# Hybrid decoder trunk: the low halves of twelve up tiles change engine, and a gate multiplication walks its operands in another order

## The chip, the cores and the metric

The kernel runs on one core of one Trainium2 chip. A time is the device time of one execution in microseconds (us), and what counts is the median of several runs. The kernel before takes 2404.12 us, the median of three runs between 2401.31 and 2413.12.

## The reference

Two layers, each a mixer followed by a PEER feed-forward block, over 256 positions of width 1024. The change touches the PEER block alone. Cut to what matters:

```
q = (xt @ w_query).reshape(T, 8, 2, 128)
s1, s2 = q[:, :, 0] @ subkeys[0].T, q[:, :, 1] @ subkeys[1].T
(v1, i1), (v2, i2) = top_k(s1, 16), top_k(s2, 16)
top, pos = top_k(all 256 sums v1 + v2, 16)
idx  = take_along_axis(i1 * 128 + i2, pos)
gate = softmax(top)
act  = gelu(einsum('thkd,td->thk', u_table[idx], x))
y    = einsum('thk,thkd->td', gate * act, v_table[idx])
```

There are 16384 experts, 128 by 128. The kernel does not gather rows of the tables: it multiplies all experts with all positions and lets the gate be zero where an expert was not chosen.

## The kernel before, in words

Products are made at more than the precision of one pass: every float32 operand is split into a high half, rounded to the multiplier's type, and a low half, the remainder, and three matmuls (high by high, low by high, high by low) stand for one product.

**Streaming (`stream`, lines 77 to 89).** Every weight tile of 128 x 1024 (512 KB) goes the same way. SyncE's queue loads it into one of four `raw` buffers; ScalarE casts it into one of three `hi` buffers (line 84); the low half, `raw - hi`, goes into one of three `lo` buffers (line 88), on the engine that the caller names. On VectorE that is one instruction of 1024 elements a partition, on GpSimd two of 512. `project` (lines 238 to 251) streams one tile and issues its 24 matmuls of 256 columns (lines 247 to 249). With three `hi` and `lo` buffers, the cast of tile n can begin only when TensorE is through with tile n-3.

**The order of the work.** The program is written for a framework that schedules: it takes the instructions as the program emits them, keeps a reckoning of its own of how long each takes, and gives each engine a fixed queue. An instruction that is emitted late may come early in its engine's queue if in that reckoning the engine has nothing earlier that is ready. On the chip each engine then runs its queue strictly in order. `tc.keep_in_program_order` holds single instructions in their program place on their engine.

**The PEER block (`peer`, lines 890 to 1059), in program order:**
- Queries: 16 tiles of `w_q`, low halves on GpSimd. After each head, `scores` (lines 928 to 942) makes the two score tables on TensorE and searches the top 16 on VectorE (lines 922 to 926, and the 16 x 16 sums of line 940).
- Up tiles: 128 tiles of `uT`, one `up(e)` for each (lines 953 to 955). `up` projects the tile and puts its Gelu (ScalarE, line 955) into `H`. Tiles 0 to 43 have their low halves on GpSimd, tiles 44 to 127 on VectorE.
- After `up(23)` the program emits the gate arithmetic on VectorE (lines 968 to 986). A softmax begins with an exponential on ScalarE (line 969, held in program order, so behind the Gelu of tile 23), whose result lines 970 to 973 use. Lines 974 to 978 take indices apart (977 and 978 convert the two index tables to float). Then come two times four rounds that look up the chosen keys: compare (line 983), multiply (line 985) and reduce (line 986), each 1024 elements a partition. All rounds use one buffer, so each of these 24 operations depends on the one before.
- `up(24)` to `up(43)`; then `sel` and the gates are transposed on TensorE (lines 989 to 995), held in program order. After that `up(44)` to `up(63)`.
- `up(64)` to `up(127)`, with `weigh(0, t8)` in between, 32 times: one-hot tables of eight positions on VectorE (lines 1011 to 1016), 16 small matmuls into a PSUM buffer (line 1020), and the multiplication of the up tiles by these gates (line 1023). `H[half]` holds 64 tiles by 256 positions a partition; line 1023 reads and writes a block of 64 tiles by 8 positions of it, so neighbouring tiles lie 256 elements apart and neighbouring positions 1. The gates in PSUM lie as 8 positions by 64 tiles.
- The accumulation over 128 tiles of `vt` (lines 253 to 277, matmuls of 512 columns in line 262), low halves on VectorE, with `weigh(1, t8)` between its first 60 steps.

Of the kernel before, what the change touches and what calls it, by code (L numbers as in the profile page):

```python
# [17 lines left out]
OP = mybir.AluOpType  # L18
# [21 lines left out]
GATE_SCALE = 2.0 ** 15  # L40
# [5 lines left out]
def trunk(ctx, tc, x, xT, w_in, w_br, w_out, w_q, skT, uT, vt, prm, lora, g2, v1, v2, rgw, w_uq, w_ukv,  # L46
          lnp, rope, out):
    nc = tc.nc
    V, A, G, T = nc.vector, nc.scalar, nc.gpsimd, nc.tensor
# [8 lines left out]
    def nm(s):  # L58
        uid[0] += 1
        return f"{s}{uid[0]}"  # L60
# [10 lines left out]
    def psm():  # L71
        return ps("sm", 2)
# [63 lines left out]
    with tc.tile_pool(name="setup", bufs=1) as sb:  # L136
        def t8(n):
            return sb.tile([P, L, 4], F32, tag=n, name=n)
        la = pr[:, :, PC["la"]:PC["la"] + 4]
        ab, e, q, w, w2, acc, rl = (t8(n) for n in ("ab", "e", "q", "w", "w2", "acc", "rl"))  # L140
# [89 lines left out]
    def drain(g):  # L230

        while True:
            try:
                next(g)
            except StopIteration as e:
                return e.value

    def project(src, eng=None):
        return drain(projecting(src, eng))

    def projecting(src, eng=None):
        hi, lo = stream(src, eng)
        h3, l3 = hi.rearrange("p (k c) -> p k c", k=8), lo.rearrange("p (k c) -> p k c", k=8)
        pt = pmm()[:, :S]
        xth, xtl = state["xth"], state["xtl"]
        for k in range(8):
            T.matmul(pt, h3[:, k, :], xth[:, k, :], start=(k == 0), stop=False)  # L247
            T.matmul(pt, h3[:, k, :], xtl[:, k, :], start=False, stop=False)  # L248
            T.matmul(pt, l3[:, k, :], xth[:, k, :], start=False, stop=(k == 7))  # L249
            yield  # L250
        return pt
# [638 lines left out]
    def peer(l, hp):  # L890
# [14 lines left out]
        H = [early.enter_context(tc.tile_pool(name=f"h{l}", bufs=1)).tile([P, 64, S], F32, tag="H0", name=nm("H"))]  # L905
# [9 lines left out]
        def nxt(k, lst):  # L915
            cyc[k] = cyc.get(k, -1) + 1
            return lst[cyc[k] % len(lst)]
# [33 lines left out]
            prev = (h, q)  # L951

        def up(e):
            p = project(uT[l, e], G if e < 44 else V)
            A.activation(H[e // 64][:, e % 64, :], p, AF.Gelu_apprx_tanh)  # L955

        up(0)
        scores(*prev)
        for e in range(1, 24):
            up(e)  # L960
# [18 lines left out]
        for f in range(2):  # L979
            for h4 in range(4):  # L980
                hs = slice(4 * h4, 4 * h4 + 4)
                t = nxt("map", maps)
# [4 lines left out]
        for e in range(24, 44):  # L987
            up(e)
        for b in range(2):
            p = psm()  # L990
# [15 lines left out]
        def weigh(half, t8):  # L1006
            oh = hp.tile([P, 8, 64, 2], F16, tag="oh", name=nm("oh"), bufs=2)
            eq = hp.tile([P, 8, 32, 2], F16, tag="eq", name=nm("eq"), bufs=2)
            go = hp.tile([P, 2, 8, 32, 2], F16, tag="go", name=nm("go"), bufs=2)
            tt = slice(8 * t8, 8 * t8 + 8)  # L1010
            V.tensor_tensor(oh, iota16[:, None].to_broadcast([P, 8, 64, 2]),  # L1011
                            ix[:, 1, tt, None, :].to_broadcast([P, 8, 64, 2]), op=OP.is_equal)
            V.tensor_tensor(eq, iota16[:, None, 32 * half:32 * half + 32].to_broadcast([P, 8, 32, 2]),
                            ix[:, 0, tt, None, :].to_broadcast([P, 8, 32, 2]), op=OP.is_equal)
            for i in range(2):
                V.tensor_tensor(go[:, i], eq, gp[:, i, tt, None, :].to_broadcast([P, 8, 32, 2]), op=OP.mult)  # L1016
            p = psm()
            for j in range(8):
                for i in range(2):
                    T.matmul(p[:, j * 64:(j + 1) * 64], oh[:, j].rearrange("p a b -> p (a b)"),  # L1020
                             go[:, i, j].rearrange("p a b -> p (a b)"), start=(i == 0), stop=(i == 1))
            hv = H[half][:, :, tt].rearrange("p e t -> p t e")
            V.scalar_tensor_tensor(hv, p.rearrange("p (t e) -> p t e", t=8), 1 / GATE_SCALE, hv, op0=OP.mult, op1=OP.mult)  # L1023

        def weigh_some(half, e):

            for t8 in range(min(e * 32 // 60, 32), min((e + 1) * 32 // 60, 32)):
                weigh(half, t8)
# [107 lines left out]
```

## Time and profile before

| | |
|---|---|
| median of 3 runs | 2404.12 us (2401.31 to 2413.12) |
| the profiled execution, its own time | 2409.22 us |
| its span in the trace | 2407.5 us |
| TensorE busy | 2264.9 us, 94% |
| VectorE busy | 1761.2 us, 73% |
| ScalarE busy | 1035.3 us, 43% |
| GpSimd busy | 679.4 us, 28% |

In the rows below PE is TensorE's matmuls, PEld its weight loads, DVE VectorE, ACT ScalarE, POOL GpSimd. "L88" is line 88 of the kernel. Times start at the beginning of the span. Matmuls are pipelined, so a busy PE says only that work was at hand.

### The profile page before, as it was taken

Reading aid. Unit: us, or ns where it says so; the run is one execution under the profiler, and the core shown is the slowest. Engines: PE = TensorE matmul, PEld = TensorE weight load, DVE = VectorE, ACT = ScalarE, POOL = GpSimd, SP = SyncE. Lnnn points to the kernel's source line nnn. Section 1 sums busy time; section 2 is a strip of 40 time slices with the busy share of each in tenths; the row PEclk is TensorE's granted clock in tenths of the full one; section 3 lists DMA queues with packets and bytes.
Section 4 is the critical chain, followed back from the end, with each engine's and each line's share of the span. In section 5 each row is a group of like instructions: output and inputs, shape, how many; then the busy total and the mean of one; then the engine's idle time right before and its main releaser. Section 6 shows DMA issues by size and latency. Waiting matters only on the chain.

```text
span 2407.5 us, 42363 instructions
## 1 busy us (share of the span) xinstructions
PE 2264.9 (94%) x17092; PEld 2066.4 (86%) x17092; DVE 1761.2 (73%) x2956; ACT 1035.3 (43%) x1461; POOL 679.4 (28%) x504
## 2 busy tenths in 40 slices
PE   6986998999999999999889869989999999999998
PEld 6886988989999988888778869889899999888886
DVE  5679487963688899855653883879636888998556
ACT  4553234444444444444345621444444444444443
POOL 4556326892000000000136653268920000000000
PEclk9998999999999999999989877999999999999999
DMA  4334243445544444655533232435455444556553
GB/s 172 106 106 140 85 170 133 168 165 186 175 160 171 169 171 173 212 199 191 185 126 131 72 130 71 169 132 173 161 188 174 166 167 167 176 175 210 193 192 140
DMA packets 104933, 382.03 MB, mean 159 GB/s; under 512 B 11648, under 2 KB 12160, under 8 KB 104480
## 3 DMA queue, kind: packets, MB, share of 16 engines
q1 hardware_dynamic: 104736, 379.32, 45.5%
q8 instruction: 134, 2.20, 0.4%
q14 instruction: 63, 0.52, 0.1%
HBM read 374.56 MB, written 4.72 MB: 158 GB/s over the span
## 4 chain that ended last, share of the span: by engine, by line
PE 82%; DVE 12%; issue 2%; POOL 2%; ACT 1%; DMA 1%; SPq 0%; DVEq 0%; POOLq 0%; ACTq 0%
PE acc L262 31%; PE mm L247 14%; PE mm L249 14%; PE mm L248 13%; PE sm L1020 2%; DVE tmp L589 2%; DVE ti L591 2%; POOL lo L88 2%; DVE lo L88 1%; PE sm L932 1%; PE acc L811 1%; DVE m L707 1%; PE acc L813 0%; PE acc L812 0%; PE acc L382 0%
## 5 line engine op out<-in xcount | busy, mean ns | idle before, releaser
L84 ACT CAST hi<-raw 128x1024 fp32r<-128x1024 f32 x658 | 689.8, 1049 | 1090.9 <-PE mm L248 359.5
L247 PE MATMUL mm<-xth,hi 128*128 128x256 f32 x3104 | 906.5, 292 | 23.0 <-ACT hi L84 11.1
L88 POOL TENSOR_TENSOR lo<-raw,hi 128x512 fp32r<-128x512 f32 x444 | 623.4, 1431 | 1025.3 <-ACT hi L84 989.2
L249 PE MATMUL mm<-xth,lo 128*128 128x256 f32 x3104 | 893.9, 288 | 12.9 <-POOL lo L88 11.3
L248 PE MATMUL mm<-xtl,hi 128*128 128x256 f32 x3104 | 892.4, 288 | 0.0
L88 DVE TENSOR_TENSOR lo<-raw,hi 128x1024 fp32r<-128x1024 f32 x436 | 533.8, 1224 | 273.4 <-ACT hi L84 272.8
L247 PEld LDWEIGHTS mm<-xth,hi 128*128 128x128 f32 x3104 | 607.9, 196 | 28.7 <-ACT g L318 11.4
L249 PEld LDWEIGHTS mm<-xth,lo 128*128 128x128 f32 x3104 | 607.7, 196 | 19.9 <-POOL lo L88 17.0
L248 PEld LDWEIGHTS mm<-xtl,hi 128*128 128x128 f32 x3104 | 608.2, 196 | 2.2 <-issue 1.0
L262 PE MATMUL acc<-hi,ah 128*128 128x512 f32 x1000 | 316.7, 396 | 0.5 <-ACT ah L166 0.5
L262 PE MATMUL acc<-lo,ah 128*128 128x512 f32 x1000 | 311.6, 391 | 0.0
L262 PE MATMUL acc<-hi,al 128*128 128x512 f32 x1000 | 310.0, 389 | 0.0
L262 PEld LDWEIGHTS acc<-hi,al 128*128 128x128 f32 x1000 | 187.7, 188 | 40.8
L262 PEld LDWEIGHTS acc<-lo,ah 128*128 128x128 f32 x1000 | 187.7, 188 | 40.4
L262 PEld LDWEIGHTS acc<-hi,ah 128*128 128x128 f32 x1000 | 183.1, 188 | 34.9 <-ACT ah L166 0.7
L1023 DVE SCALAR_TENSOR_TENSOR H<-sm,H 128x512 f32<-128x512 f32 x128 | 171.1, 1337 | 56.2 <-PE sm L1020 56.1
L167 DVE SCALAR_TENSOR_TENSOR al<-H,ah 128x1024 fp32r<-128x1024 f32 x64 | 78.3, 1224 | 33.8 <-ACT ah L166 33.8
L166 ACT ACTIVATE ah<-H 128x1024 fp32r<-128x1024 f32 x64 | 67.9, 1061 | 81.7 <-PE acc L262 77.0
L1016 DVE TENSOR_TENSOR go<-eq,gp 128x512 f16<-128x512 f16 x256 | 97.3, 419 | 0.0
L955 ACT ACTIVATE H<-mm 128x256 f32<-128x256 f32 x256 | 96.5, 377 | 0.0
L1011 DVE TENSOR_TENSOR oh<-iota,ix 128x1024 f16<-128x1024 f16 x128 | 87.7, 685 | 2.3 <-PE sm L1020 2.3
L1020 PEld LDWEIGHTS <-oh 128*128 128x128 f16 x2048 | 66.7, 98 | 19.1 <-issue 13.6
(353 smaller groups left out, 2169.2 us busy)
## 6 DMA issues: line engine op xcount, KB each, us to landing
raw<-in_uT_dram SPq DMA_DIRECT2D x256, 512.0 KB, 3.2
raw<-in_vt_dram SPq DMA_DIRECT2D x256, 512.0 KB, 3.3
raw<-in_w_in_dram SPq DMA_DIRECT2D x100, 512.0 KB, 3.3
raw<-in_w_q_dram SPq DMA_DIRECT2D x32, 512.0 KB, 3.2
raw<-in_w_br_dram SPq DMA_DIRECT2D x24, 512.0 KB, 3.3
raw<-in_w_out_dram SPq DMA_DIRECT2D x16, 512.0 KB, 3.4
ln<-in_lnp_dram SPq DMA_DIRECT2D x8, 512.0 KB, 5.1
xd<-ln SPq DMA_DIRECT2D x6, 512.0 KB, 2.6
```

The costliest lines, as they stand in the source:

```text
L84: A.copy(hi, raw)
L88: eng.tensor_sub(lo[:, c:c + n], raw[:, c:c + n], hi[:, c:c + n].bitcast(F32))
L167: V.scalar_tensor_tensor(lo, src, scale, hi.bitcast(F32), op0=OP.mult, op1=OP.subtract)
L247: T.matmul(pt, h3[:, k, :], xth[:, k, :], start=(k == 0), stop=False)
L248: T.matmul(pt, h3[:, k, :], xtl[:, k, :], start=False, stop=False)
L249: T.matmul(pt, l3[:, k, :], xth[:, k, :], start=False, stop=(k == 7))
L262: T.matmul(acc[b][hf], m[:, bs], w[:, 512 * hf:512 * hf + 512], start=(k == 0 and j == 0), stop=(k == n - 1 and j == 2))
L955: A.activation(H[e // 64][:, e % 64, :], p, AF.Gelu_apprx_tanh)
L1011: V.tensor_tensor(oh, iota16[:, None].to_broadcast([P, 8, 64, 2]), ix[:, 1, tt, None, :].to_broadcast([P, 8, 64, 2]), op=OP.is_equal)
L1016: V.tensor_tensor(go[:, i], eq, gp[:, i, tt, None, :].to_broadcast([P, 8, 32, 2]), op=OP.mult)
L1020: T.matmul(p[:, j * 64:(j + 1) * 64], oh[:, j].rearrange("p a b -> p (a b)"), go[:, i, j].rearrange("p a b -> p (a b)"), start=(i == 0), s ...
L1023: V.scalar_tensor_tensor(hv, p.rearrange("p (t e) -> p t e", t=8), 1 / GATE_SCALE, hv, op0=OP.mult, op1=OP.mult)
```

## The change

`up` names VectorE instead of GpSimd for the low half of tiles 20, 22, ... 42. Line 1023 does the same multiplication on the same elements, but its operands are walked tile by tile with the eight positions innermost, where before they were walked position by position with the 64 tiles innermost.

```
@@ -951,7 +951,7 @@
         def up(e):
-            p = project(uT[l, e], G if e < 44 else V)
+            p = project(uT[l, e], G if e < 20 or (e < 44 and e % 2) else V)
             A.activation(H[e // 64][:, e % 64, :], p, AF.Gelu_apprx_tanh)
@@ -1019,8 +1019,8 @@
-            hv = H[half][:, :, tt].rearrange("p e t -> p t e")
-            V.scalar_tensor_tensor(hv, p.rearrange("p (t e) -> p t e", t=8), 1 / GATE_SCALE, hv, op0=OP.mult, op1=OP.mult)
+            hv = H[half][:, :, tt]
+            V.scalar_tensor_tensor(hv, p.rearrange("p (t e) -> p e t", t=8), 1 / GATE_SCALE, hv, op0=OP.mult, op1=OP.mult)
```

## Rows read from the trace of the kernel before

**Rows 1.** The page, part 4: the chain that ended last, by engine and line.

```profile
PE 82%; DVE 12%; issue 2%; POOL 2%; ACT 1%; DMA 1%; SPq 0%; DVEq 0%; POOLq 0%; ACTq 0%
PE acc L262 31%; PE mm L247 14%; PE mm L249 14%; PE mm L248 13%; PE sm L1020 2%; DVE tmp L589 2%; DVE ti L591 2%; POOL lo L88 2%; DVE lo L88 1%; PE sm L932 1%; PE acc L811 1%; DVE m L707 1%; PE acc L813 0%; PE acc L812 0%; PE acc L382 0%
```

**Rows 2.** Waits, 440 to 600 us: us in total, times, longest.

```profile
PEld mm L249 <- POOL lo L88: 7.5, 12, 0.7
```

**Rows 3.** ScalarE in order of time, layer 0: start, us, work [idle before].

```profile
481.26 1.06 ACT L84 CAST hi<-raw 128x1024 fp32r<-128x1024 f32 x1 [1.55 <-PE mm L249]
...
502.49 1.05 ACT L84 CAST hi<-raw 128x1024 fp32r<-128x1024 f32 x1 [2.34 <-PE mm L249]
...
505.13 0.42 ACT L969 ACTIVATE tk<-tk 128x256 f32<-128x256 f32 x1
...
526.78 1.05 ACT L84 CAST hi<-raw 128x1024 fp32r<-128x1024 f32 x1 [1.55 <-POOL lo L88]
...
558.47 1.05 ACT L84 CAST hi<-raw 128x1024 fp32r<-128x1024 f32 x1 [1.55 <-PE mm L249]
```

**Rows 4.** The same view, layer 1.

```profile
1689.33 1.05 ACT L84 CAST hi<-raw 128x1024 fp32r<-128x1024 f32 x1 [1.55 <-PE mm L249]
...
1731.97 1.05 ACT L84 CAST hi<-raw 128x1024 fp32r<-128x1024 f32 x1 [1.55 <-POOL lo L88]
```

**Rows 5.** Groups, 470 to 518 us: shapes, count | busy us, mean ns | idle before.

```profile
L88 POOL TENSOR_TENSOR lo<-raw,hi 128x512 fp32r<-128x512 f32 x27 | 49.6, 1873 | 0.2 <-ACT hi L84 0.2
...
L983 DVE TENSOR_TENSOR tk<-tk,iota 128x1024 f32<-128x1024 f32 x8 | 17.6, 2200 | 0.3
...
L986 DVE TENSOR_REDUCE tk<-tk 128x64 f32<-128x1024 f32 x8 | 9.8, 1220 | 0.3
```

**Rows 6.** VectorE in order of time, 462 to 560 us.

```profile
462.87 0.80 DVE L977 CAST tk<-tk 128x256 f32<-128x256 uint32 x1
463.59 0.28 DVE L925 MAX8 tk<-tk 128x8 f32<-128x128 f32 x1
...
470.98 2.25 DVE L983 TENSOR_TENSOR tk<-tk,iota 128x1024 f32<-128x1024 f32 x1
...
515.48 1.22 DVE L986 TENSOR_REDUCE tk<-tk 128x64 f32<-128x1024 f32 x1
516.62 0.41 DVE L970 TENSOR_REDUCE gsm<-tk 128x16 f32<-128x256 f32 x1
...
559.55 1.23 DVE L88 TENSOR_TENSOR lo<-raw,hi 128x1024 fp32r<-128x1024 f32 x1 [40.17 <-ACT hi L84]
```

**Rows 7.** Groups, 524 to 540 us, GpSimd.

```profile
L88 POOL TENSOR_TENSOR lo<-raw,hi 128x512 fp32r<-128x512 f32 x14 | 17.6, 1302 | 0.1
```

**Rows 8.** Groups of VectorE over the whole span.

```profile
L88 DVE TENSOR_TENSOR lo<-raw,hi 128x1024 fp32r<-128x1024 f32 x436 | 533.8, 1224 | 273.4 <-ACT hi L84 272.8
L1023 DVE SCALAR_TENSOR_TENSOR H<-sm,H 128x512 f32<-128x512 f32 x128 | 171.1, 1337 | 56.2 <-PE sm L1020 56.1
...
L940 DVE TENSOR_TENSOR tk<-tk 128x256 f32<-128x256 f32 x32 | 26.0, 812 | 0.0
...
L922 DVE MAX8 tk<-tk 128x8 f32<-128x256 f32 x32 | 13.2, 413 | 0.1
...
L185 DVE SCALAR_TENSOR_TENSOR ln<-ln,acc 128x512 f32<-128x512 f32 x16 | 11.0, 686 | 25.4 <-PE acc L262 25.4
```

**Rows 9.** The page, part 6: DMA issues, KB each, us to landing.

```profile
raw<-in_uT_dram SPq DMA_DIRECT2D x256, 512.0 KB, 3.2
```

**Rows 10.** Windows around the layer norm: PE, PEld, DVE, ACT, POOL busy; PEclk, DMA, GB/s.

```profile
368.00:372.00 4.00, 0.00 (x0) 0.00 (x0) 3.89 (x9) 0.00 (x0) 1.94 (x2) 0.50 0.54 204
374.00:378.00 4.00, 4.00 (x20) 3.54 (x19) 1.61 (x3) 1.19 (x2) 0.00 (x0) 0.58 0.43 164
```

**Rows 11.** Windows, same columns, in the two stages that run line 1023.

```profile
660.00:720.00 60.00, 60.00 (x622) 59.57 (x618) 52.27 (x70) 24.96 (x38) 0.00 (x0) 1.00 0.48 167
840.00:900.00 60.00, 60.00 (x399) 48.24 (x397) 58.62 (x79) 25.51 (x25) 0.00 (x0) 1.00 0.51 176
```

## The prediction

> **What bounds the kernel now.** The profiled execution took 2409.22 us around a span of 2407.5; the median of the three runs shown is 2404.12, 5 us less. Differences below are worked out in the profiled execution and then set against the median.
>
> I read the chain of waits first: 82% of what ended last is TensorE [rows 1], so a faster VectorE or GpSimd is worth something only where TensorE waits for it. GpSimd has 2% of the chain, its low halves (line 88) [rows 1]. The view of waits places them: in the stretch from 440 to 600 us of layer 0 TensorE's weight loads wait 12 times for a low half of GpSimd [rows 2]. ScalarE's order of time gives the size. VectorE's first low half of an up tile, at 559.55, is tile 44 [rows 6], so the cast at 558.47 is tile 44's, and counting back, one cast per tile, 481.26 is tile 20's and 526.78 tile 33's [rows 3]. With three hi buffers the cast of tile n starts when TensorE has finished tile n-3, so casts show TensorE's pace: from tile 33 to 44 it is 31.69 / 11 = 2.88 us a tile, from 20 to 33 it is 45.52 / 13 = 3.50. The loss is 45.52 - 13 x 2.88 = **8.1 us**; layer 1 repeats it from tile 21 to 33, 1731.97 - 1689.33 = 42.64 for twelve tiles [rows 4]. So 16.1 us of 2409 is all that the first edit can win.
>
> Why there: in this stretch VectorE works through eight rounds of compare, multiply and reduce (lines 983, 985, 986), 24 operations in a row. The two-input ones take 2.20 us with GpSimd beside them, and GpSimd's half tile 1.87 [rows 5]; later, with VectorE idle, the half tile takes 1.30 [rows 7], and a low half of the same 1024 elements on VectorE 1.22 in the mean [rows 8]. They take turns. Two half tiles at 1.87 make 3.75 us, above the 2.88 that TensorE needs.
>
> **The first edit: twelve even tiles (20 to 42) change engine, in each layer.** GpSimd loses 24 half tiles per layer and keeps one tile in two: 3.75 us at its slowest per 5.76, no longer late. VectorE gains 12 x 1.22 = 14.7 us. From 519.4 it is idle for 40.17 us [rows 6], which covers the low halves of tiles 32 to 42; they cost nothing. No transfer changes; but the load of tile 24 now waits for VectorE to release tile 20's raw buffer. It lands 3.2 us after issue [rows 9], ahead of the cast of tile 24 in every case below.
>
> What counts is where tiles 20 to 30 fall in VectorE's queue, for it is in order. The order is the scheduler's: line 977, late in the program, runs between operations of a dependent top-16 search [rows 6], so whatever is ready in the scheduler's reckoning goes into the next gap. A low half stands behind as many of the 24 operations as the scheduler believes done when the tile's cast is done. Call this n for tile 20. The trace does not show n; I bound it.
> - From below: line 970 comes before these rounds in the program but runs behind the last of them (516.62 after 515.48) [rows 6]. Its input, the exponential (505.13), is held behind the Gelu of tile 23 [rows 3], so in the reckoning the rounds were issued before the exponential was done. At an unhindered pace the cast of tile 20 ends at 482.3, that of tile 26 starts at 481.26 + 6 x 2.88 = 498.5 and the exponential ends 3.1 later, as it did after 502.49: 501.6. These 19.3 us hold 15 operations at 1.26 (1.22 and the gap between dependent ones). So n is at least 9, if the scheduler's engines stand to each other as the unhindered rows do.
> - From above nothing: the rounds may be over before tile 20 (n = 24).
> - Likeliest: the scheduler knows no turn-taking. Line 940, hindered, takes 0.81 us where an operation of its size takes 0.41 [rows 8]; 16 of them per layer put the rounds 6.4 us later than reckoned. It sees them begin at 470.98 - 6.4 = 464.6 [rows 6], and at 482.3 it has done 17.7 / 1.26 = **14**. Each later even tile follows 5.76 us on, of which 1.22 is a low half: 4 operations further (18, 22, then behind the rounds).
>
> On the chip, n = 14: TensorE wants tile 20 at 481.26 + 2 x 2.88 = 487.0. From 470.98 a round takes 5.7 us beside GpSimd; without tile 20 GpSimd has ten half tiles (16 to 19 and 21) of 1.87 from 470.9 on, is done with tile 21 at 489.6 and runs out, since tile 23's cast needs tile 20's buffer. By then 9.7 operations are done; the other 4.3 take 5.4 us, the low half 1.2: 496.2. TensorE waits 9.2 us. It then runs at half clock: in the layer-norm gap the granted clock fell to 0.50 (1.2 GHz) with the engine idle, and it was 0.58 in the mean of the first 4 us of full work after it [rows 10], so 4 x 0.42 = 1.7 us more. Tiles 22 and 24 follow within about a tile pair each; 1 us for both. The slowness of tile 19, still on GpSimd, leaves 0.4. Sum 12.3 against 8.1: **+4.2 us a layer, +8 in all**. The map operations behind a waiting low half have cover: their result is first read after tile 43.
>
> With n = 9: the third round ends at 488.1, so tile 20 is 2.3 us late, and 22, 24 and 26 some 2 each, because GpSimd keeps taking turns; about 9, or +1 a layer. With n = 18: 9.2 + 4 x 1.26 = 14.2 of waiting, 17 with the rest, +9 a layer. So this case spans +2 to +18.
>
> **The second edit: line 1023 walks tile by tile.** Now it takes 1.337 us for 512 elements, both SBUF operands hopping 256 elements; afterwards they come in runs of 8 and the PSUM operand hops by 64. The same operation with all operands contiguous takes 0.686 (line 185) [rows 8]. No row has VectorE hopping in PSUM; between 0.686 and 1.337, I take 0.8, nearer the contiguous row because two of three operands become runs. Dearer than 1.337 is not excluded (a rival below). On the path I cost it at nothing: where it runs TensorE is busy all 60 us of 660 to 720 and of 840 to 900, with VectorE at 52.27 and 58.62 [rows 11]; that PE work is the cover. About 128 x 0.5 = 70 us of VectorE time becomes idle time.
>
> [...]
>
> **The rivals.**
> - *The low halves interleave well* (the scheduler's rounds are slower, or TensorE faster, than I read). For it: nothing in VectorE's total forbids it, 24 x 1.22 us being all that is added. Against: the bound n of 9. With tile 20 in time, each even tile still shares turns: -8 to -16, 2388 to 2396. Chance 0.25.
> - *VectorE's queue becomes the wait* (slower). Place: the low half of tile 20 behind the 24 operations or nearly. Point: n above 18. At n = 24, 14.3 x 1.26 = 18.0 us after 489.6, and 1.2: late by 21.8, with the clock and tile 19 23.9 against 8.1, +15.8 a layer, 2436; at n = 20, +11 a layer, 2426. For it: the scheduler's rounds had ended before the exponential, by how much is not shown. Against: my start at 464.6. Chance 0.23.
> - *The hop in PSUM is dear.* From 840 to 900 VectorE has 1.38 us of idle for about 10.7 of these operations (32 in 60 tiles, a tile some 3 us), 0.13 each; beyond 1.47 us VectorE ends the accumulation's step. At 2.0 us, 32 times 0.53 a layer: +34 in all, 2438. Against: VectorE's contiguous PSUM row at 0.686 is no dearer than SBUF. Chance 0.05.
>
> [...]
>
> **How the numbers follow.** Forecast case (n from 9 to 18) 0.47, at n = 14: 2404.1 + 8 = 2412. About 0.5% (12 us) is what a measurement of this kernel can tell from no change. Of the forecast case 0.36 lies within that (up to n = 15) and 0.11 above; the good interleaving gives 0.20 faster and 0.05 within; the two slower rivals 0.28. So faster 0.20, same 0.41, slower 0.39. The forecast case alone is 2406 to 2422; as cases of both signs hold much chance, the range reaches into them, 2393 to 2430, leaving out the lower edge of the good case and the upper ends of the slower ones, together 0.2.
>
> **What would show it.** Right: from tile 20 on GpSimd's half tiles near 1.3 us outside the rounds and no wait of TensorE for it; a single long wait of TensorE for VectorE's low half at tile 20 in each layer, about 9 us, and a granted clock below 1.0 after it; line 1023 near 0.8 us with TensorE still full from 600 to 1160. Wrong: low halves spread through the rounds from the third on, with casts every 2.88 us (faster); the first of them behind line 986's last (slower); line 1023 above 1.47 us.

## The result, and the profile after

The changed kernel takes **2445.11 us** (median of 4 runs, 2440.43 to 2453.02) beside 2408.62 us for the kernel before (median of 4, 2401.31 to 2419.84): ratio **1.014**, 95% interval 1.0107 to 1.0174. This ratio, like those below, is the one on record and not the quotient of the two medians, which is 1.015. The change is slower by 1.4%, outside the predicted range. The profiled execution has a span of 2443.1 us against 2407.5.

The place is found with two landmarks in each layer: the first query copy (line 948) and the first gate matmul (line 1020), which stands right behind the stretch of up tiles. Columns: duration in ns as least, median, most; first and last start in us. First the kernel before, then the changed one, layer 0:

```profile
L948 ACT COPY tk<-mm x16: 364/366/369, 380.3 to 429.5; 128x256 f32<-128x256 f32 x16
L1020 PE MATMUL sm<-go,oh x1024: 193/193/203, 628.0 to 1007.3; 128*128 128x64 f16 x171
```

```profile
L948 ACT COPY tk<-mm x16: 366/367/368, 383.0 to 432.2; 128x256 f32<-128x256 f32 x16
L1020 PE MATMUL sm<-go,oh x1024: 193/193/203, 647.0 to 1026.3; 128*128 128x64 f16 x171
```

From copy to matmul it is 247.7 us before and 264.0 after: **+16.3**; layer 1 gives 247.8 and 264.1. The stretch of gate matmuls that follows, where the second edit sits, takes 379.3 us in both. So all of it lies between the queries and the end of the up tiles, twice. What is left of the 35.6 us between the spans is 2.7 at the start and 0.3 in between.

The chain by engine, against [rows 1], shows VectorE with 22% where it had 12:

```profile
PE 73%; DVE 22%; issue 2%; ACT 2%; POOL 0%; DMA 0%; SPq 0%; DVEq 0%; ACTq 0%; POOLq 0%
```

The waits from 440 to 600 us, against the twelve short ones of [rows 2] (us in total, times, longest):

```profile
ACT hi L84 <- PE mm L248: 47.0, 16, 25.1
...
PEld mm L249 <- DVE lo L88: 21.8, 1, 21.8
PE mm L249 <- DVE lo L88: 21.6, 1, 21.6
```

One wait of TensorE for one low half on VectorE, seen once by its matmuls and once by its weight loads; layer 1 has the same wait, 21.6 and 21.8. VectorE in order of time shows which one and why, against [rows 6]:

```profile
473.70 2.26 DVE L983 TENSOR_TENSOR tk<-tk,iota 128x1024 f32<-128x1024 f32 x1
...
490.95 2.16 DVE L983 TENSOR_TENSOR tk<-tk,iota 128x1024 f32<-128x1024 f32 x1
493.14 1.22 DVE L985 TENSOR_TENSOR tk<-tk 128x1024 f32<-128x1024 f32 x1
...
509.50 1.22 DVE L986 TENSOR_REDUCE tk<-tk 128x64 f32<-128x1024 f32 x1
510.63 2.35 DVE L88 TENSOR_TENSOR lo<-raw,hi 128x1024 fp32r<-128x1024 f32 x2
520.66 1.23 DVE L88 TENSOR_TENSOR lo<-raw,hi 128x1024 fp32r<-128x1024 f32 x1 [7.68 <-ACT hi L84]
...
528.43 0.42 DVE L970 TENSOR_REDUCE gsm<-tk 128x16 f32<-128x256 f32 x1 [0.79 <-ACT tk L969]
```

All 24 round operations run first, from 473.70 to the one of line 986 at 509.50, and then tiles 20 and 22 together. In the terms of the prediction n is **24**. GpSimd meanwhile runs dry (start, us, work, idle before):

```profile
473.59 18.44 POOL L88 TENSOR_TENSOR lo<-raw,hi 128x512 fp32r<-128x512 f32 x10 [0.21 <-ACT hi L84]
...
517.69 2.56 POOL L88 TENSOR_TENSOR lo<-raw,hi 128x512 fp32r<-128x512 f32 x2 [25.66 <-ACT hi L84]
```

Its ten half tiles, 1.84 us each, end at 492.0; from 493.14 on VectorE's two-input operations take 1.22 instead of 2.2. ScalarE's casts give TensorE's pace, against [rows 3]:

```profile
483.99 1.06 ACT L84 CAST hi<-raw 128x1024 fp32r<-128x1024 f32 x1 [1.55 <-PE mm L249]
...
490.15 1.04 ACT L84 CAST hi<-raw 128x1024 fp32r<-128x1024 f32 x1 [1.95 <-PE mm L249]
516.57 1.05 ACT L84 CAST hi<-raw 128x1024 fp32r<-128x1024 f32 x1 [25.09 <-PE mm L248]
...
545.66 1.05 ACT L84 CAST hi<-raw 128x1024 fp32r<-128x1024 f32 x1 [1.42 <-PE mm L248]
```

483.99 is tile 20, 490.15 tile 22, 516.57 tile 23 and 545.66 tile 33. The loss is 545.66 - 483.99 - 13 x 2.88 = 24.2 us, where it was 8.1: 16.1 more, the landmarks' 16.3.

Windows (length, PE, PEld, DVE, ACT, POOL busy; PEclk, DMA, GB/s), two behind the wait and the two of [rows 11]:

```profile
512.00:516.00 4.00, 4.00 (x19) 4.00 (x20) 0.98 (x1) 0.00 (x0) 0.00 (x0) 0.50 0.76 271
516.00:520.00 4.00, 4.00 (x35) 4.00 (x35) 0.00 (x0) 1.75 (x3) 2.31 (x2) 0.98 0.34 126
...
660.00:720.00 60.00, 60.00 (x613) 59.57 (x610) 46.16 (x69) 25.03 (x39) 0.00 (x0) 1.00 0.51 168
840.00:900.00 60.00, 59.77 (x398) 48.99 (x398) 50.66 (x71) 27.31 (x28) 0.00 (x0) 1.00 0.54 174
```

The granted clock is 0.50 in the first 4 us of work behind the wait, where neighbouring matmuls of 256 columns start 0.213 us apart (1.2 columns a ns), and 0.98 in the next 4, where from 516.13 on they start 0.120 apart. Where line 1023 runs, VectorE has 6 to 8 us less work per 60, and TensorE is as full as before but for 0.23 us. The group of line 1023, against [rows 8]:

```profile
L1023 DVE SCALAR_TENSOR_TENSOR H<-sm,H 128x512 f32<-128x512 f32 x128 | 88.3, 690 | 85.1 <-PE sm L1020 84.4
```

0.690 us instead of 1.337: VectorE lost 83 us of work, and nothing came of it.

### The profile page after: what moved, and what is told of

The parts are those of the page before. It is cut to its first block, busy times and chain, and to the rows that moved or that the text cites. A ratio compares the mean times of both kernels' runs of the same rounds, so it can differ in the third digit from the quotient of the medians.

```text
span 2443.1 us, 42327 instructions
## 1 busy us (share of the span) xinstructions
PE 2264.7 (93%) x17092; PEld 2069.9 (85%) x17092; DVE 1701.1 (70%) x2980; ACT 1035.7 (42%) x1461; POOL 600.6 (25%) x456
## 4 chain that ended last, share of the span: by engine, by line
PE 73%; DVE 22%; issue 2%; ACT 2%; POOL 0%; DMA 0%; SPq 0%; DVEq 0%; ACTq 0%; POOLq 0%
PE acc L262 30%; PE mm L247 11%; PE mm L249 11%; PE mm L248 11%; PE sm L1020 2%; DVE tmp L589 2%; DVE ti L591 2%; DVE tk L926 1%; DVE tk L923 1%; DVE tk L924 1%; DVE tk L983 1%; DVE tk L985 1%; DVE tk L940 1%; DVE tk L922 1%; DVE tk L925 1%
## 5 line engine op out<-in xcount | busy, mean ns | idle before, releaser
L88 POOL TENSOR_TENSOR lo<-raw,hi 128x512 fp32r<-128x512 f32 x396 | 544.1, 1398 | 1137.9 <-ACT hi L84 1098.2
L88 DVE TENSOR_TENSOR lo<-raw,hi 128x1024 fp32r<-128x1024 f32 x460 | 563.4, 1225 | 328.5 <-ACT hi L84 327.9
L1023 DVE SCALAR_TENSOR_TENSOR H<-sm,H 128x512 f32<-128x512 f32 x128 | 88.3, 690 | 85.1 <-PE sm L1020 84.4
```

The source lines that it names most:

```text
L88: eng.tensor_sub(lo[:, c:c + n], raw[:, c:c + n], hi[:, c:c + n].bitcast(F32))
L1023: V.scalar_tensor_tensor(hv, p.rearrange("p (t e) -> p e t", t=8), 1 / GATE_SCALE, hv, op0=OP.mult, op1=OP.mult)
```

## The experiments

The theory after the result (**queue**): a low half on VectorE costs only what stands before it in VectorE's queue, and the scheduler put all 24 round operations before tile 20's. The rivals: the **walk** of the second edit has a part in the loss; or a low half on VectorE costs TensorE time **wherever it stands**.

"Stretch" below is the time from the first query copy to the first gate matmul in the profiled execution, layer 0 / layer 1. In kernels whose order is held by hand the lines are shifted: 93 is `lo` (88 before), 985, 988 and 990 are the round operations (983, 985, 986), 1001 or 1004 the exponential (969), 1005 or 1007 the gate sum (970).

| kernel | ratio to before, 95% interval | stretch, us |
|---|---|---|
| before | 1 | 247.7 / 247.8 |
| after | 1.0140 (1.0107 to 1.0174) | 264.0 / 264.1 |
| first edit alone | 1.0141 (1.0108 to 1.0174) | 264.4 / 264.2 |
| second edit alone | 1.0015 (0.9997 to 1.0033) | 247.8 / 247.8 |
| even tiles from 32 only | 0.9998 (0.9984 to 1.0013) | 247.8 / 247.8 |
| markers | one run, 2469.81 us | 275.3 / 275.3 |
| 14 operations first, exponential late | 1.0069 (1.0040 to 1.0097) | 258.1 / 259.3 |
| 14 operations first | 1.0080 (1.0058 to 1.0102) | 255.1 / 254.1 |
| 7 operations first | 0.9944 (0.9923 to 0.9965) | 240.4 / 240.4 |
| all on VectorE, exponential late | 0.9988 (0.9969 to 1.0007) | 247.5 / 247.5 |
| all on VectorE | 0.9925 (0.9900 to 0.9950); 0.9894 (0.9877 to 0.9911) | 239.9 / 239.9 |
| all on VectorE, new walk | 0.9885 (0.9862 to 0.9908); 0.9902 (0.9885 to 0.9918) | 239.8 / 239.9 |

**One edit at a time.** First edit alone:

```
-            p = project(uT[l, e], G if e < 44 else V)
+            p = project(uT[l, e], G if e < 20 or (e < 44 and e % 2) else V)
```

> The twelve even tiles change engine, line 1023 walks as before. Queue theory (all the time is lost because the low half of tile 20 stands behind all 24 round operations in VectorE's queue): as slow as the whole change, +33 us (1.2 to 1.6% slower), TensorE waiting once per layer about 22 us for that low half; line 1023 stays at 1.34 us. Walk theory (the new walk of line 1023 costs part of it, by itself or by shifting the queue): clearly less than +33 us.

Second edit alone:

```
-            hv = H[half][:, :, tt].rearrange("p e t -> p t e")
+            hv = H[half][:, :, tt]
```

with the PSUM operand rearranged to match.

> Only line 1023 walks tile by tile. Queue theory: no change, within 0.3% of the kernel before, though VectorE loses 128 x 0.65 = 83 us of busy time (line 1023 at 0.69 us), since TensorE is full where it runs. Walk theory: slower by 5 us or more. A third possibility, that VectorE at 58 of 60 us held TensorE back in the accumulation: faster by 5 to 15 us, the stretch between the first and the last of line 1020 shorter than before.

The first has the whole loss, 2444.58 us and ratio 1.0141; the second is within 0.35% of no change, with the stretch as before. The walk is out as a cause of the loss.

**Only where VectorE is idle.** The condition is `e < 32 or (e < 44 and e % 2)`.

> The first edit for the tiles after the rounds only: even tiles from 32 to 42 on VectorE, 20 to 30 left on GpSimd. The queue theory: VectorE is idle there (40 us in the kernel before), so these low halves cost nothing and win nothing: TensorE's loss of 8.1 us a layer lies at tiles 20 to 33, and the time is that of the kernel before within 0.3%. The rival, that a low half on VectorE costs TensorE time wherever it stands: half of the change's loss, ratio near 1.007.

Measured 0.9998, and GpSimd's twelve waits of [rows 2] are there unchanged (7.5 us). Low halves behind the rounds cost nothing: "wherever it stands" falls here already.

**Where the scheduler believes the rounds to be.** Six early tiles serve as markers, with the order left to the scheduler:

```
+            p = project(uT[l, e], G if e < 44 and e not in (2, 5, 8, 11, 14, 17) else V)
```

> The kernel before with six early tiles as markers: the low halves of tiles 2, 5, 8, 11, 14 and 17 on VectorE, its order left to the scheduler. Where each stands in VectorE's queue shows what the scheduler believes done when that tile's cast is done. My prediction had the rounds beginning 6.4 us earlier than on the chip, some six tiles before tile 20's cast ends: then the markers of tiles 2 to 11 stand before the first round operation, that of tile 14 about at it, and tile 17 behind some 7 operations. If the scheduler believes the searches over much earlier, as the queue of the changed kernel says (tile 20 behind all 24), the markers of tiles 11 and 14 already stand among the rounds, 6 or 7 operations apart (three tiles of 2.88 us, less a low half of 1.22, at 1.26 an operation), and the first round operation lies at tile 9 or earlier. TensorE then waits for VectorE's searches at the first markers, so the time is of no interest: slower by 20 us or more a layer by the late start, by less if only the markers after tile 11 are late.

VectorE in order of time, layer 0, with the operations between left out:

```profile
466.90 1.22 DVE L88 TENSOR_TENSOR lo<-raw,hi 128x1024 fp32r<-128x1024 f32 x1
468.24 0.27 DVE L977 CAST tk<-tk 128x256 f32<-128x256 uint32 x1
...
471.48 0.41 DVE L968 TENSOR_TENSOR tk<-tk 128x256 f32<-128x256 f32 x1
...
472.79 1.22 DVE L983 TENSOR_TENSOR tk<-tk,iota 128x1024 f32<-128x1024 f32 x1
473.93 1.22 DVE L88 TENSOR_TENSOR lo<-raw,hi 128x1024 fp32r<-128x1024 f32 x1
...
484.43 1.22 DVE L88 TENSOR_TENSOR lo<-raw,hi 128x1024 fp32r<-128x1024 f32 x1
...
497.00 2.28 DVE L88 TENSOR_TENSOR lo<-raw,hi 128x1024 fp32r<-128x1024 f32 x1
...
507.69 2.32 DVE L88 TENSOR_TENSOR lo<-raw,hi 128x1024 fp32r<-128x1024 f32 x1
...
518.17 1.23 DVE L88 TENSOR_TENSOR lo<-raw,hi 128x1024 fp32r<-128x1024 f32 x1
```

GpSimd in the same stretch, its first work after the end of the one before at 444.6:

```profile
476.08 2.61 POOL L88 TENSOR_TENSOR lo<-raw,hi 128x512 fp32r<-128x512 f32 x2 [31.45 <-ACT hi L84]
```

The low half of tile 2 stands between the last searches. That of tile 5 stands behind one round operation, tile 8 behind 7, tile 11 behind 13, tile 14 behind 19, tile 17 behind all 24. Two things are read from it. The pace is six operations in three tiles, four to a pair, as the prediction had it. The start is not: in the scheduler's reckoning one operation is done when the cast of tile 5 is, 15 tiles or 43.2 us before that of tile 20, so the rounds begin at about 482.3 - 43.2 - 1.3 = 438 on the clock of the kernel before (an estimate, from its 2.88 us a tile), where the chip began them at 470.98.

Turn-taking, by which no more is meant than the rows give (line 983 at 2.20 us beside GpSimd [rows 5], 1.22 here at 472.79 with GpSimd idle), explains the smaller part of these 33 us. Here GpSimd stood still from 444.6 to 476.1 us, held up by tile 2, and the first round starts 472.79 - 386.1 = 86.7 us after this kernel's first query copy, 4.0 less than the 90.7 of the kernel before. Ahead of 444.6 turns still cost line 940 some 4.3 us (its 16 operations take 10.7 us in all, at 0.40 each 6.4), and tile 2's own low half takes 1.1. Without either the rounds would begin 81.3 us after the first copy, at about 461.6 on the clock of the kernel before (an estimate). So turns are worth some 9 us, where the prediction had 6.4, and some 24 us lie in the reckoning itself: in what it takes a search to cost, or in how soon it has the tiles come. Which, no trace shows, and no kernel was made to find out.

**The forecast case itself.** VectorE's order is held by hand with `tc.keep_in_program_order` around each low half and each of the 24 operations (`ops` yields them one by one), so that tile 20 stands behind 14 of them and each later even tile 4 further:

```
+        for e in range(20, 44):
+            for _ in range(14 if e == 20 else 4 if e % 2 == 0 else 0):
...
+                next(ops, None)
...
+            up(e)
...
```

> The engines as in the change, line 1023 as before, but VectorE's order is held by hand to what the prediction took for likeliest: 14 round operations, low half of tile 20, then 4 operations before each of tiles 22 and 24, the rest before 26. If only the place in the queue was wrong, the prediction's own sum holds here: TensorE waits 9 to 10 us for tile 20, +4 us a layer, +6 to +11 us in all (0.2 to 0.5% slower). Rival (a low half on VectorE costs TensorE time wherever it stands): +20 us or more.

The ratio, 1.0069, is some +17 us rather than 6 to 11, but the rewrite had brought a wait of its own: it moved the exponential behind tile 30, and VectorE, in order, stood there.

```profile
DVE gsm L1005 <- ACT tk L1004: 9.3, 1, 9.3
```

So the run was made again with the exponential behind tile 23 and the gate sum behind tile 36.

> The changed engines with VectorE's order held by hand as the forecast case had it: 14 of the 24 round operations, the low half of tile 20, 4 operations, tile 22, 4, tile 24, 2, tile 26, and so on. Unlike the run before it, the exponential stays behind the Gelu of tile 23, where the kernel before has it, and the gate sum stands behind the low half of tile 36, so that VectorE does not wait for the exponential. My prediction's sum: +4.2 us a layer, +8 in all, ratio 1.0035. The trace of the run before says that the second term was too small: there tile 20 was late by about 9.2 us as reckoned, but tile 24 by another 5, not 1 for both tiles. If that is right and only the 2.8 us at the exponential go, +6 to +7 a layer, +12 to +14, ratio 1.005 to 1.006. If it stays at 1.007, the exponential was not the reason for the rest.

That wait is gone, and the stretch grows by 7.4 and 6.3 us, where the prediction's sum said 4.2. The time itself did not fall: the ratio is 1.0080, beside 1.0069 with the wait (the intervals overlap), and by the expectation's own sign the exponential would not have been the reason for the rest. The profiles say that it was a part of it, since the stretches are 3.0 and 5.2 us shorter than with the wait. TensorE's longest wait for a low half is the reckoned one (us in total, times, longest):

```profile
PE mm L254 <- DVE lo L93: 11.6, 2, 9.0
```

ScalarE's casts of tiles 22, 23, 26 and 27:

```profile
492.33 1.04 ACT L89 CAST hi<-raw 128x1024 fp32r<-128x1024 f32 x1 [1.95 <-PE mm L254]
...
505.80 1.05 ACT L89 CAST hi<-raw 128x1024 fp32r<-128x1024 f32 x1 [12.14 <-PE mm L253]
...
514.56 1.04 ACT L89 CAST hi<-raw 128x1024 fp32r<-128x1024 f32 x1 [1.68 <-PE mm L254]
...
521.25 1.05 ACT L89 CAST hi<-raw 128x1024 fp32r<-128x1024 f32 x1 [3.63 <-PE mm L253]
```

Tile 20's wait costs 505.80 - 492.33 - 2.88 = 10.6 us, where the sum had 9.2 for the wait and 1.7 for the clock. Tile 24's costs 521.25 - 514.56 - 2.88 = 3.8, where the sum had 1 for two tiles. VectorE's rows say why:

```profile
506.28 1.22 DVE L93 TENSOR_TENSOR lo<-raw,hi 128x1024 fp32r<-128x1024 f32 x1
507.41 2.32 DVE L985 TENSOR_TENSOR tk<-tk,iota 128x1024 f32<-128x1024 f32 x1
509.76 2.20 DVE L988 TENSOR_TENSOR tk<-tk 128x1024 f32<-128x1024 f32 x1
...
513.26 1.80 DVE L985 TENSOR_TENSOR tk<-tk,iota 128x1024 f32<-128x1024 f32 x1
514.98 2.28 DVE L93 TENSOR_TENSOR lo<-raw,hi 128x1024 fp32r<-128x1024 f32 x1
```

506.28 is the low half of tile 22, 514.98 that of tile 24. Once tile 20 is through, GpSimd has work again, and the three two-input operations of the four ahead of tile 24 take turns with it, at 2.32, 2.20 and 1.80 us; so does tile 24's low half, at 2.28. By the median (+17.6 us of 2413.38) the run came out dearer than the 12 to 14 expected, by the landmarks (+13.7 together) as expected; the expectation's ratio lies at the lower end of the interval.

**The same engines, only earlier in the queue.** Seven operations, tile 20, then two operations before each later even tile.

> The changed engines exactly (even tiles from 20 to 42 on VectorE), order held by hand: 7 round operations, then the low half of tile 20, and two operations between it and each later one; exponential behind the Gelu of tile 23, gate sum behind the low half of tile 40. The queue theory: tile 20 is in time (7 operations end near 485, wanted at 487), the odd tiles on GpSimd have 5.76 us for 3.75, and VectorE's two operations at 2.2 and a low half fill 5.6 of 5.76: casts near 2.88 us a tile, half or more of the 8.1 us a layer gained, -8 to -16, ratio 0.993 to 0.997. The rival, that the low half on VectorE is slow beside GpSimd wherever it stands: waits of TensorE for it at many tiles, ratio 1.000 or more.

Ratio 0.9944, and the stretch is 7.3 us shorter in the first layer and 7.4 in the second. Tile 20's low half ends at 492.75, when TensorE wants it (its cast starts at 487.07, and 2 x 2.88 later is 492.83), and from 440 to 600 us TensorE waits for one low half only, a GpSimd one:

```profile
490.44 2.31 DVE L93 TENSOR_TENSOR lo<-raw,hi 128x1024 fp32r<-128x1024 f32 x1
```

```profile
PEld mm L254 <- POOL lo L93: 0.3, 1, 0.3
```

These are the engines of the change, tile for tile; what differs is VectorE's order. The sign of the first edit hangs on that order.

**All low halves from tile 16 on VectorE**, one between every two round operations, so that GpSimd is out and no turns are taken. First with the exponential late:

> All low halves from tile 16 on are on VectorE, held by hand in turn with the rounds: one round operation, one low half, and so on; GpSimd has no part in this stretch. Line 1023 as before. Queue theory: 1.22 + 1.26 = 2.48 us of VectorE per tile of 2.88, no turns to take with GpSimd, so TensorE never waits: the 8.1 us a layer that the kernel before loses are gone, -16 us (0.6 to 0.7% faster). Rival (a low half on VectorE costs TensorE time wherever it stands): slower than before, since 28 tiles a layer are there instead of 12.

Ratio 0.9988: the casts ran at 2.88 us up to tile 43, and the gain went at the exponential, since the gate sum, and behind it the low halves of tiles 41 to 43, waited 9.4 us for it. With the exponential back behind tile 23 and the gate sum behind tile 40:

> All low halves from tile 16 on VectorE, one between every two round operations, order held by hand; the exponential behind the Gelu of tile 23 and the gate sum behind the low half of tile 40, so that VectorE waits for it nowhere. The theory that the cost of a low half on VectorE is only what it stands behind in the queue: TensorE goes at 2.88 us a tile from 16 to 44, nothing of the 8.1 us a layer is left and none comes back, -16 us, ratio 0.993. The rival, that moving low halves to VectorE beside the rounds costs TensorE time wherever they stand (a port, the number of waits): no gain or a loss, ratio 1.000 or more, as it was with the exponential late.

VectorE in order of time, and no wait in it but for casts:

```profile
500.66 1.22 DVE L985 TENSOR_TENSOR tk<-tk,iota 128x1024 f32<-128x1024 f32 x1
502.39 1.23 DVE L93 TENSOR_TENSOR lo<-raw,hi 128x1024 fp32r<-128x1024 f32 x1 [0.52 <-ACT hi L89]
503.54 1.22 DVE L988 TENSOR_TENSOR tk<-tk 128x1024 f32<-128x1024 f32 x1
505.27 1.23 DVE L93 TENSOR_TENSOR lo<-raw,hi 128x1024 fp32r<-128x1024 f32 x1 [0.52 <-ACT hi L89]
```

An operation and a low half, 1.22 each, fit into a tile's 2.88 us with 0.4 to spare. The stretch is 7.8 us shorter, 0.3 short of all that was lost.

With the new walk, and both kernels measured a second time beside each other:

> As the kernel sent with it (all low halves from tile 16 on VectorE in a held order), with the second edit too: line 1023's operation walks tile by tile. The theory that the second edit lies wholly beside TensorE: the same time as its sister within 0.2%, ratio 0.993. The rival, that the walk's 70 us of VectorE time are worth something once nothing else delays TensorE, or that its hop in PSUM costs: more than 0.3% from its sister.

> All low halves from tile 16 on VectorE in a held order, line 1023's operation with its old walk: a second measurement beside its sister with the new walk, on one chip. The theory that the walk lies beside TensorE: 0.993 again, the same as the sister within 0.2%. The other: the sister faster by 0.3% or more, as in the first measurement (0.9885 against 0.9925, intervals that touch).

> The sister with the new walk. The theory that the walk lies beside TensorE: 0.993, within 0.2% of the kernel with the old walk. The other: 0.3% or more below it, 0.989 or less.

The first pair, 0.9925 and 0.9885, looked like 0.4% for the walk; the second, 0.9894 and 0.9902, has the other sign. The stretches agree to 0.1 us. No worth of the walk shows here either. By the ratios both versions are about 1% faster than the kernel before and, ratio against ratio, 2 to 2.5% faster than the change; how much of the 1% is TensorE's clock is said in the last section.

## Why the prediction was wrong

- **The budget was right.** 8.1 us a layer was all there was to win: the best order gets 7.8 of it back.
- **What the edit costs away from the rounds was right:** nothing from tile 32 on (0.9998). The load of tile 24 was no matter either: its cast, at 519.58, waited for TensorE. So were the turns: 2.2 us with GpSimd at work, 1.22 from 493.14 on, when it has none.
- **The step that failed** is "It sees them begin at 470.98 - 6.4 = 464.6 [rows 6], and at 482.3 it has done 17.7 / 1.26 = **14**". It took the scheduler's reckoning to be the chip's own times with the turn-taking out. The markers put the beginning of the rounds at about 438 in that reckoning, and the changed kernel has tile 20 behind all 24. Taking the turns out, even in full, would have moved the start only to about 461.6 and n to 20.7 / 1.26 = 16. What makes the reckoning earlier by the other 24 us stays open. The bound from below, n of at least 9, held; the point "From above nothing" said that n = 24 was open. The evidence for it stood in the rival, as "by how much is not shown", and was outweighed by a start that rested on one correction.
- **The pace was right**, four operations to a tile pair.
- **The price of the rival was right.** At n = 24 the prediction has tile 20 late by 21.8 us, 23.9 lost and +15.8 a layer; the profile has a wait of 21.6 (21.8 for the weight load), 24.2 lost and +16.3. The rival's 2436 is 32 us above its median of before; measured are 36.5 between the medians and 34 by the ratio. Its sign, the first low half behind line 986's last, is what the trace shows. It had a chance of 0.23, and the range ended below it.
- **The forecast case was underpriced.** Set up by hand it costs 7.4 and 6.3 us more a layer by the landmarks, not 4.2; the wait for tile 20 itself, 9.0, is as reckoned. The term "Tiles 22 and 24 follow within about a tile pair each; 1 us for both" left out that the turns come back when GpSimd has work again: 3.8 for tile 24.
- **The second edit was right:** nothing on the path, and line 1023 at 0.690 us, near the contiguous 0.686 of [rows 8] rather than at the 0.8 taken. With runs of 8 in SBUF and a hop of 64 in PSUM it costs 0.004 us over the contiguous row; the dear hop of the rival is not there.

## What to carry to other kernels

When work moves to an engine that runs its queue in order, its price is what stands before it in that queue, at the pace that the other engines leave it: TensorE's wait for tile 20 was 21.6 us behind 24 operations, 9.0 behind 14, and none behind 7. If a scheduler writes the queue, its reckoning may be off from the chip's times, here by some 33 us (an estimate, from the markers); a few markers, instructions whose place is free, read it out of one trace. Where the place decides the sign, hold the order by hand, and then look for what the held order itself makes wait, as the exponential did here (9.3 us).

## What had not been expected of the hardware

The all-VectorE kernels gain more than the tiles give: with the old walk the profiled spans differ by 23.6 us, of which 15.7 lie in the two stretches, and 13.6 between them, less 5.7 for a later start. Of the 13.6 us 11.7 lie behind a gap in the mixer of layer 1, and they go with TensorE's clock. In that gap TensorE stands idle for some 18 us beside a chain on VectorE (17.9 in the kernel before and in the changed one), and the granted clock falls to 0.50 there in the kernel before, the changed one, the one with the first edit alone, and the all-VectorE kernels with the old walk and with the new. How long it stays there differs. Windows, same columns as above, of the kernel before, then of the all-VectorE kernel with the old walk:

```profile
1430.00:1434.00 4.00, 0.00 (x0) 0.00 (x0) 3.97 (x5) 0.00 (x0) 0.00 (x0) 0.50 0.00 0
1438.00:1442.00 4.00, 4.00 (x27) 3.44 (x25) 0.59 (x2) 0.85 (x2) 2.50 (x2) 0.50 0.00 0
1462.00:1466.00 4.00, 4.00 (x29) 3.43 (x28) 0.31 (x2) 1.33 (x2) 1.68 (x2) 0.50 0.01 2
1470.00:1474.00 4.00, 4.00 (x46) 3.73 (x45) 1.39 (x2) 1.33 (x2) 1.18 (x1) 1.00 0.01 4
```

```profile
1427.90:1431.90 4.00, 0.56 (x9) 0.50 (x9) 3.92 (x7) 0.00 (x0) 0.00 (x0) 0.50 0.00 0
1435.90:1439.90 4.00, 4.00 (x39) 3.50 (x37) 0.89 (x3) 0.00 (x0) 1.22 (x1) 0.78 0.37 131
1459.90:1463.90 4.00, 4.00 (x61) 3.80 (x61) 1.81 (x3) 0.00 (x0) 0.09 (x1) 1.00 0.38 131
```

In the first the clock is still 0.50 over 25 us after TensorE took up work again (at 1435.35), in the second it is back at 1.00 within 10 (work from 1431.34, a mean of 1.00 from 1439.90 to 1443.90), with the same work ahead. From there to the first query copy the one takes 150.1 us at a mean granted clock of 0.85, the other 138.4 at 0.94. The kernel with the first edit alone lies between (951.1 us from layer 0's first gate matmul to layer 1's first query copy, against 957.4 and 943.8). One and the same kernel, all on VectorE with the new walk, has 944.7 in one profile and 951.7 in another, on another chip, so the kernel alone does not fix this time.

Executions on one chip differ as well, for each run has its mean granted clock on record, and within each kernel a lower clock goes with a longer time. Of the 13 runs of the kernel before on one chip, the two at 0.971 took 2404.47 and 2404.89 us, the one at 0.968 2405.17 and the one at 0.961 2420.84. Of the six of the all-VectorE kernel with the old walk beside them, the one at 0.970 took 2385.64, the four at 0.968 2390.23 to 2392.53, and the one at 0.962 2403.49. At like clocks the two kernels are thus 13 to 19 us apart, around the 15.7 us of the stretches; what the ratios show beyond that goes with the clock. Three of the four profiles of these kernels have the short way from layer 0's first gate matmul to layer 1's first query copy (943.8, 944.2 and 944.7 us, against 951.7); why stays open. That is why the ratios of these kernels are read beside their stretches.
